# Splitting the last row of a ReLU row sum into three column pieces instead of two

## The chip, the cores and the metric

The kernel runs on one core of a Trainium2 chip. The metric is the time of one execution on the device in microseconds (us). Besides it each run lists its **span**: the time from the program's first to its last instruction in the profile, rounded to 0.1 us. In the lines of the profile DVE is VectorE, ACT is ScalarE, SPq is SyncE's queue, and L102 is line 102 of the kernel that ran. All runs told of here were in the fast state, with a granted clock of 1.00.

## The reference

```python
x = np.random.randn(32, 512, 1024).astype(np.float32)
def reference(x):
    return np.sum(np.maximum(x, 0), axis=-1).astype(np.float32)
```

There are 16384 rows of 1024 numbers, 67 MB, and one number comes out per row. Each of the 128 partitions takes 128 rows.

## The kernel before

SyncE issues all loads on one queue: seven chunks of 16 rows per partition, then a tail that gets smaller (8, 4, 2 and 1 rows), then the last row in two halves. Six chunks are worked on in three steps, ScalarE applying the ReLU and VectorE summing the rows. From the seventh on (and for four rows of the sixth) the engines share the rows: each takes every second one and does both the ReLU and the sum in one call, which becomes an arithmetic instruction and an accumulator read (for a full row 1215 and 83 ns on VectorE, 1044 and 186 ns on ScalarE, means of the trace).

```python
def on_act(t, acc):
    return act.activation(t, t, AF.Relu, accum_out=acc)
def on_dve(t, acc):
    return dve.tensor_scalar(out=t, in0=t, scalar1=0.0, scalar2=None,
                             op0=ALU.max, op1=ALU.add, accum_out=acc)
# ... six chunks in three steps ...
        for i, n in enumerate(steps):
            t = buf[:, b, r : r + n, :]
            act.activation(t, t, AF.Relu).then_inc(s_act, 1)
            dve.wait_ge(s_act, 3 * c + i + 1)
            dve.tensor_reduce(out=res[...], in_=t, axis=X, op=ALU.add).then_inc(s_dve, 1)
# ... the seventh chunk ...
        for i in range(BIG):
            ins = (on_act if i % 2 else on_dve)(*row(c, i))
# ... the tails of 8, 4, 2, 1; then the last row ...
    act.wait_ge(s_in[-2], 16)
    on_act(buf[:, tb, BIG - 1, 0 : LAST[0]], last[:, LAST[1] : LAST[1] + 1]).then_inc(s_tact, 1)
    dve.wait_ge(s_tact, 1)
    dve.wait_ge(s_in[-1], 16)
    on_dve(last[:, :], res[:, J - 1 : J]).then_inc(s_tdve, 1)
    sp.wait_ge(s_tdve, 1)
    sp.dma_start(out=ov[-1][:, :], in_=res[:, start[-1] : J]).then_inc(s_out, 16)
```

ScalarE sums the first half of the last row and puts the sum, which can't be negative, into the column behind the second half. VectorE's last instruction then sums 512 + 1 numbers, and the final store follows.

Of the kernel before, what the change touches and what calls it, by code (L numbers as in the profile page):

```python
# [2 lines left out]

P = 128
D = 1024
BIG = 16
NTWO = 6
NB = 3
REGIONS = [112, 16]
CHUNKS = [(0, 0), (0, 16), (0, 32), (0, 48), (0, 64), (0, 80), (0, 96)]  # L10
STEPS = [4, 5, 7]
MIXED = [3, 4, 5]
TAIL = [8, 4, 2, 1]
LAST = [512, 512]


def bass_relu_sum_kernel(
    nc: bass.Bass,
    x: bass.AP,
    out: bass.AP,  # L20
):







    fp32 = mybir.dt.float32
    ALU = mybir.AluOpType  # L30
    AF = mybir.ActivationFunctionType
    X = mybir.AxisListType.X

    B, S, _ = x.shape
    J = B * S // P
    NBIG = len(CHUNKS)
    assert BIG * NBIG + sum(TAIL) + 1 == J == sum(REGIONS) and sum(LAST) == D

    xr = x.rearrange("b s d -> (b s) d")
    of = out.rearrange("b s -> (b s)")  # L40
    start = [sum(REGIONS[:i]) for i in range(len(REGIONS))]
    xv = [
        xr[P * s : P * (s + n), :].rearrange("(p j) d -> p j d", p=P)
        for s, n in zip(start, REGIONS)
    ]
    ov = [of[P * s : P * (s + n)].rearrange("(p j) -> p j", p=P) for s, n in zip(start, REGIONS)]

    buf = nc.alloc_sbuf_tensor("buf", [P, NB, BIG, D], fp32)
    last = nc.alloc_sbuf_tensor("last", [P, LAST[1] + 1], fp32)
    res = nc.alloc_sbuf_tensor("res", [P, J], fp32)  # L50

    n_in = NBIG + len(TAIL) + 2
    s_in = [nc.alloc_semaphore(f"s_in{i}") for i in range(n_in)]
    s_act = nc.alloc_semaphore("s_act")
    s_dve = nc.alloc_semaphore("s_dve")
    s_fact = nc.alloc_semaphore("s_fact")
    s_fdve = nc.alloc_semaphore("s_fdve")
    s_tact = nc.alloc_semaphore("s_tact")
    s_tdve = nc.alloc_semaphore("s_tdve")
    s_store = nc.alloc_semaphore("s_store")  # L60
    s_out = nc.alloc_semaphore("s_out")

    sp, act, dve = nc.sync, nc.scalar, nc.vector


    tb = NBIG % NB
    for c in range(NBIG + 1):
        if c >= NB:
            sp.wait_ge(s_dve, 3 * (c - NB + 1))
        if c < NBIG:  # L70
            g, j = CHUNKS[c]
            sp.dma_start(out=buf[:, c % NB, :, :], in_=xv[g][:, j : j + BIG, :]).then_inc(  # L72
                s_in[c], 16
            )
    r = 0
    tail = []
    for i, n in enumerate(TAIL):
        sp.dma_start(out=buf[:, tb, r : r + n, :], in_=xv[-1][:, r : r + n, :]).then_inc(  # L78
            s_in[NBIG + i], 16
        )  # L80
        tail.append((r, n, s_in[NBIG + i]))
        r += n
    sp.dma_start(out=buf[:, tb, r, 0 : LAST[0]], in_=xv[-1][:, BIG - 1, 0 : LAST[0]]).then_inc(
        s_in[-2], 16
    )
    sp.dma_start(out=last[:, 0 : LAST[1]], in_=xv[-1][:, BIG - 1, LAST[0] : D]).then_inc(
        s_in[-1], 16
    )
    sp.wait_ge(s_fact, 1)
    sp.wait_ge(s_fdve, 1)  # L90
    for g in range(len(REGIONS) - 1):
        sp.dma_start(
            out=ov[g][:, :], in_=res[:, start[g] : start[g] + REGIONS[g]]
        ).then_inc(s_store, 16)
# [6 lines that stand above are left out]
        return dve.tensor_scalar(  # L101
            out=t, in0=t, scalar1=0.0, scalar2=None, op0=ALU.max, op1=ALU.add, accum_out=acc  # L102
        )

    def row(c, i):
        return buf[:, c % NB, i, :], res[:, c * BIG + i : c * BIG + i + 1]

    for c in range(NTWO):
        b, steps = c % NB, STEPS if c < NTWO - 1 else MIXED
        act.wait_ge(s_in[c], 16)  # L110
        if steps is MIXED:
            dve.wait_ge(s_in[c], 16)
            for i in (BIG - 4, BIG - 3):
                on_dve(*row(c, i))
        r = 0
# [4 lines that stand above are left out]
            dve.tensor_reduce(  # L120
                out=res[:, c * BIG + r : c * BIG + r + n], in_=t, axis=X, op=ALU.add
            ).then_inc(s_dve, 1)
            r += n
        if steps is MIXED:
            for i in (BIG - 2, BIG - 1):
                on_act(*row(c, i))


    j0 = NBIG * BIG
    for c in range(NTWO, NBIG):  # L130
        act.wait_ge(s_in[c], 16)
        dve.wait_ge(s_in[c], 16)
        for i in range(BIG):
            ins = (on_act if i % 2 else on_dve)(*row(c, i))
            if i >= BIG - 2:
                ins.then_inc(s_fact if i % 2 else s_fdve, 1)
    for r, n, s in tail:
        if n > 1:
            act.wait_ge(s, 16)
        dve.wait_ge(s, 16)  # L140
        for i in range(r, r + n):
            f = on_act if (i - r) % 2 else on_dve
            f(buf[:, tb, i, :], res[:, j0 + i : j0 + i + 1])

    act.wait_ge(s_in[-2], 16)
    on_act(buf[:, tb, BIG - 1, 0 : LAST[0]], last[:, LAST[1] : LAST[1] + 1]).then_inc(s_tact, 1)
    dve.wait_ge(s_tact, 1)
    dve.wait_ge(s_in[-1], 16)
    on_dve(last[:, :], res[:, J - 1 : J]).then_inc(s_tdve, 1)


    sp.wait_ge(s_tdve, 1)
    sp.dma_start(out=ov[-1][:, :], in_=res[:, start[-1] : J]).then_inc(s_out, 16)
    sp.wait_ge(s_store, 16 * (len(REGIONS) - 1))
    sp.wait_ge(s_out, 16)


# [1 line left out]
_INS = ['x']  # L159
_OUTS = [((32, 512), 'float32')]  # L160


# [21 lines left out]
```

## Time and profile before

| What | Before |
|---|---|
| Time, the three runs known at first | 162.46 to 162.5 us, median 162.47 |
| Profiled run | 162.37 us, span 160.7 us |
| Load queue's share of the span | 97.4% |
| VectorE, ScalarE busy | 76%, 63% |
| From VectorE's last full row to the final store | 2.16 us (157.09 to 159.25) |

With the load queue at 97.4% of the span the load stream sets the time, and behind it stands a short tail. The last row of the table is the measure for that tail. It starts at an event just after the landing of the last full row, so it does not depend on when the loads as a whole come to an end.

### The profile page before, as it was taken

To read this page: it belongs to the slowest core of one execution; us is meant where nothing else is said; L and a number is where in the kernel's file an instruction comes from. 1 tells how busy PE (TensorE), PEld (TensorE's weight loads), DVE (VectorE), ACT (ScalarE), POOL (GpSimd) and SP (SyncE) were. 2 spreads that over 40 slices of the span, in tenths; PEclk is the share of its full clock that TensorE was granted. 3 is DMA by queue.
4 is the path that set the end of the run, shared out by engine and by line. 5 is a ranking of instruction groups with operands and counts; after the bars stand their busy time and mean duration, and the time that the engine had idled before them with its cause. 6 is when DMAs were issued, how large, how long until landed. Compare 5 with 4: busy or idle time off the path is not lost.

```text
span 160.7 us, 145 instructions
## 1 busy us (share of the span) xinstructions
DVE 122.0 (76%) x56; ACT 101.0 (63%) x55; POOL 0.2 (0%) x4
## 2 busy tenths in 40 slices
DVE  0000004998969898898969989699899999598995
ACT  3000039991599907997099951999329980496972
POOL 0000000000000000000000000000000000000000
DMA  8969969969969969969969969969969969899993
GB/s 261 522 261 522 522 261 522 522 261 522 522 261 522 522 261 522 522 261 522 522 261 522 522 261 522 522 261 522 522 261 522 506 277 522 367 416 391 418 399 113
DMA packets 2160, 67.18 MB, mean 418 GB/s; under 512 B 496, under 2 KB 496, under 8 KB 880
## 3 DMA queue, kind: packets, MB, share of 16 engines
q1 hardware_dynamic: 2160, 67.18, 97.4%
HBM read 67.11 MB, written 0.07 MB: 418 GB/s over the span
## 4 chain that ended last, share of the span: by engine, by line
DMA 69%; ACT 18%; DVE 10%; SPq 1%; issue 0%
DMA buf<-in_x_dram 69%; ACT buf L118 17%; DVE res L120 9%; SPq L78 1%; ACT buf L98 0%; DVE last L101 0%; SPq L72 0%
## 5 line engine op out<-in xcount | busy, mean ns | idle before, releaser
L120 DVE TENSOR_REDUCE res<-buf 128x4 f32<-128x4096 f32 (+3 forms) x18 | 100.4, 5604 | 34.3 <-ACT buf L118 34.3
L118 ACT ACTIVATE buf<-buf 128x4096 f32<-128x4096 f32 (+3 forms) x18 | 80.8, 4553 | 47.1 <-DMA buf<-in_x_dram 47.1
L98 ACT ACTIVATE buf<-buf 128x1024 f32<-128x1024 f32 (+1 forms) x18 | 18.4, 1021 | 9.7 <-DMA buf<-in_x_dram 9.7
L101 DVE TENSOR_SCALAR_CACHE_REDUCE buf<-buf 128x1024 f32<-128x1024 f32 x18 | 21.0, 1215 | 2.7 <-DMA buf<-in_x_dram 2.5
L98 ACT ACTIVATION_READ_ACCUMULATOR buf<-buf 128x1 f32 x18 | 3.4, 186 | 0.0
L118 ACT ACT_TABLE_LOAD x1 | 1.3, 1283 | 0.7 <-PEq L169 0.7
L101 DVE DVE_READ_ACCUMULATOR buf<-buf 128x1 f32 x18 | 1.5, 83 | 0.0
L101 DVE TENSOR_SCALAR_CACHE_REDUCE last<-last 128x513 f32<-128x513 f32 x1 | 0.7, 690 | 0.2 <-ACT buf L98 0.2
L169 POOL MEMSET const-bfloat16-1.0<- 128x1 bf16 x1 | 0.1, 102 | 0.0
L169 POOL MEMSET const-uint8-127<- 128x1 uint8 x1 | 0.1, 102 | 0.0
L169 POOL MEMSET const-float32-0.0<- 128x1 f32 x1 | 0.1, 99 | 0.2 <-issue 0.2
L169 POOL MEMSET const-float32-1.0<- 128x1 f32 x1 | 0.1, 99 | 0.0
L101 DVE DVE_READ_ACCUMULATOR last<-last 128x1 f32 x1 | 0.1, 83 | 0.0
## 6 DMA issues: line engine op xcount, KB each, us to landing
buf<-in_x_dram SPq DMA_DIRECT2D x1, 4096.0 KB, 26.7
buf<-in_x_dram SPq DMA_DIRECT2D x1, 2048.0 KB, 31.2
buf<-in_x_dram SPq DMA_DIRECT2D x1, 1024.0 KB, 33.2
buf<-in_x_dram SPq DMA_DIRECT2D x1, 512.0 KB, 34.0
buf<-in_x_dram SPq DMA_DIRECT2D x1, 256.0 KB, 34.2
last<-in_x_dram SPq DMA_DIRECT2D x1, 256.0 KB, 34.3
buf<-in_x_dram SPq DMA_DIRECT2D x7, 36.3
out_dram<-res SPq DMA_DIRECT2D x1, 56.0 KB, 10.6
```

Source lines behind the costliest of these rows:

```text
L78: sp.dma_start(out=buf[:, tb, r : r + n, :], in_=xv[-1][:, r : r + n, :]).then_inc(s_in[NBIG + i], 16)
L98: return act.activation(t, t, AF.Relu, accum_out=acc)
L101: return dve.tensor_scalar(out=t, in0=t, scalar1=0.0, scalar2=None, op0=ALU.max, op1=ALU.add, accum_out=acc)
L118: act.activation(t, t, AF.Relu).then_inc(s_act, 1)
L120: dve.tensor_reduce(out=res[:, c * BIG + r : c * BIG + r + n], in_=t, axis=X, op=ALU.add).then_inc(s_dve, 1)
L169: nc = _bacc.Bacc("TRN2", target_bir_lowering=False, num_devices=1)
```

## The change

The intent is to let VectorE start on the last row while ScalarE still works, and to make VectorE's last instruction short. The row arrives as 576, 256 and 192 columns. ScalarE sums the first piece and VectorE the second. VectorE's last instruction sums the third together with the two partial sums.

```diff
-LAST = [512, 512]
+LAST = [576, 256, 192]
...
-    last = nc.alloc_sbuf_tensor("last", [P, LAST[1] + 1], fp32)
+    last = nc.alloc_sbuf_tensor("last", [P, LAST[2] + 2], fp32)
...
+    s_tpart = nc.alloc_semaphore("s_tpart")
... (three loads in place of two, each with its own semaphore)
-    act.wait_ge(s_in[-2], 16)
-    on_act(buf[:, tb, BIG - 1, 0 : LAST[0]], last[:, LAST[1] : LAST[1] + 1]).then_inc(s_tact, 1)
+    n = LAST[2]
+    act.wait_ge(s_in[-3], 16)
+    on_act(parts[0], last[:, n : n + 1]).then_inc(s_tact, 1)
+    dve.wait_ge(s_in[-2], 16)
+    on_dve(parts[1], last[:, n + 1 : n + 2]).then_inc(s_tpart, 1)
+    dve.wait_ge(s_in[-1], 16)
+    dve.wait_ge(s_tpart, 1)
     dve.wait_ge(s_tact, 1)
-    dve.wait_ge(s_in[-1], 16)
     on_dve(last[:, :], res[:, J - 1 : J]).then_inc(s_tdve, 1)
```

More of the change, by code (lines that the diff above doesn't have):

```diff
@@ L48, in bass_relu_sum_kernel @@
     buf = nc.alloc_sbuf_tensor("buf", [P, NB, BIG, D], fp32)
-    last = nc.alloc_sbuf_tensor("last", [P, LAST[1] + 1], fp32)
+    last = nc.alloc_sbuf_tensor("last", [P, LAST[2] + 2], fp32)
     res = nc.alloc_sbuf_tensor("res", [P, J], fp32)
-    n_in = NBIG + len(TAIL) + 2
+    n_in = NBIG + len(TAIL) + len(LAST)
     s_in = [nc.alloc_semaphore(f"s_in{i}") for i in range(n_in)]
@@ L82, in bass_relu_sum_kernel @@
         r += n
-    sp.dma_start(out=buf[:, tb, r, 0 : LAST[0]], in_=xv[-1][:, BIG - 1, 0 : LAST[0]]).then_inc(
-        s_in[-2], 16
-    )
-    sp.dma_start(out=last[:, 0 : LAST[1]], in_=xv[-1][:, BIG - 1, LAST[0] : D]).then_inc(
-        s_in[-1], 16
-    )
+    n0, n1 = LAST[0], LAST[0] + LAST[1]
+    parts = [buf[:, tb, r, 0:n0], buf[:, tb, r, n0:n1], last[:, 0 : LAST[2]]]
+    for k, (lo, hi) in enumerate([(0, n0), (n0, n1), (n1, D)]):
+        sp.dma_start(out=parts[k], in_=xv[-1][:, BIG - 1, lo:hi]).then_inc(
+            s_in[NBIG + len(TAIL) + k], 16
+        )
     sp.wait_ge(s_fact, 1)
```

## The prediction

> **What bounds the kernel now.** I read the page first, for the busy shares and the chain that ended last, then the chain in order of time, and then the timeline of the last microseconds, because the change touches nothing earlier than those. In the page the reader is to see that no compute engine is full (VectorE 76%, ScalarE 63%), while the DMA engines are busy in every slice and the load queue fills 97.4% of the span.
>
> ```profile
> DVE 122.0 (76%) x56; ACT 101.0 (63%) x55; POOL 0.2 (0%) x4
> q1 hardware_dynamic: 2160, 67.18, 97.4%
> HBM read 67.11 MB, written 0.07 MB: 418 GB/s over the span
> ```
>
> So the 67 MB of input set the time. The change moves not a byte of that. What it can touch is the stretch from the landing of the last input to the end. The chain in order of time shows its steps: the last load of the chain lands at 157.74, ScalarE takes 0.73 us for its half row, VectorE 0.69 us for the other half.
>
> ```profile
> 123.55 34.19 DMA buf<-in_x_dram
> 157.74 0.02 issue
> 157.76 0.73 ACT buf L98 x2
> 158.49 0.03 issue
> 158.53 0.69 DVE last L101 x2
> ```
>
> The timeline shows the same stretch with VectorE's row before it, and the store that ends the program.
>
> ```profile
> 157.09 1.22 DVE L101 TENSOR_SCALAR_CACHE_REDUCE buf<-buf 128x1024 f32<-128x1024 f32 x1
> 157.76 0.63 ACT L98 ACTIVATE buf<-buf 128x512 f32<-128x512 f32 x1 [0.83 <-DMA buf<-in_x_dram]
> 158.24 0.08 DVE L101 DVE_READ_ACCUMULATOR buf<-buf 128x1 f32 x1
> 158.30 0.18 ACT L98 ACTIVATION_READ_ACCUMULATOR buf<-buf 128x1 f32 x1
> 158.53 0.69 DVE L101 TENSOR_SCALAR_CACHE_REDUCE last<-last 128x513 f32<-128x513 f32 x1 [0.21 <-ACT buf L98]
> 159.14 0.08 DVE L101 DVE_READ_ACCUMULATOR last<-last 128x1 f32 x1
> 159.25 0.34 SPq L153 DMA_DIRECT2D out_dram<-res  x1
> ```
>
> VectorE is free of its last full row at 158.32 and idles 0.21 us for ScalarE's partial sum. It ends at 159.14 + 0.08 = 159.22; the store is issued at 159.25, takes 1.4 us to land and closes the span. That store is the same in both kernels.
>
> When do the pieces land? Issue times are in the chain (121.71, 122.08, 122.56 and 123.06 for the tails of 8, 4, 2 and 1 rows, 123.55 for the first half) and in the timeline (124.08 for the second half); the DMA view has the time to landing. The sums are 148.4, 153.3, 155.8, 157.06, 157.74 and 158.4. So the second half lands only some 0.1 us before ScalarE's sum is there: transfer and ScalarE are almost balanced already.
>
> ```profile
> buf<-in_x_dram SPq DMA_DIRECT2D x1, 512.0 KB, 34.0
> buf<-in_x_dram SPq DMA_DIRECT2D x1, 256.0 KB, 34.2
> last<-in_x_dram SPq DMA_DIRECT2D x1, 256.0 KB, 34.3
> ```
>
> [...] six loads on one queue, in issue order, and the store of the first 112 results, issued at 147.99 behind them, needs 10.6 us, to about 158.6, just after the last load. [...] one row takes 1.30 us (155.76 to 157.06), half a row 0.68 and then about 0.65. A straight line through 1.30 and 0.68 is 0.62 us per half row plus 0.06 us per transfer; through two rows (2.48) and one (1.30) it is 0.59 plus 0.12. [...] the trace has 1057 ns for 1024 elements after a wait and 629 for 512, that is 428/512 = 0.836 ns. [...]
>
> **The change part by part.**
>
> *Transfers.* One load more on the same queue, its issue (0.44 us of SyncE near 124.5) 33 us before it matters: nothing. Landing, with 0.08 us per transfer and 0.60 us per half row (both chosen between the two lines above): 576 columns 0.08 + 0.675 = 0.76, so 157.82 instead of 157.74; 256 columns 0.08 + 0.30 = 0.38, so 158.20; 192 columns 0.08 + 0.225 = 0.31, so 158.50 instead of 158.4. All input arrives about 0.1 us later.
>
> *ScalarE.* 64 columns more at 0.836 ns is 0.05 us, so 0.78 us for the pair instead of 0.73. Start 157.84, end 158.62, and with the 0.04 us that the trace has from ScalarE's end to VectorE's start, VectorE could go on at 158.66 instead of 158.53. On the path: 0.13 us later.
>
> *VectorE, middle piece.* VectorE's cost per element: 1215 ns for 1024 and 690 for 513 make 525/511 = 1.03 ns. For 256 elements 690 - 257 x 1.03 = 425 ns, up to the end of its accumulator read. It can start when piece two is there (158.22 with the hand-over) and the row before is done. In the trace rows follow each other every 1.14 us, so 157.09 + 1.14 = 158.23. Both come at about the same moment: start 158.25, end 158.67. This fills the 0.21 us in which VectorE idled, and some more.
>
> *VectorE, last piece.* It waits for three things: data (158.50), ScalarE (158.66), its own partial sum (158.67 + 0.04 = 158.71, if a VectorE wait on VectorE costs what the ScalarE hand-over costs). The last is the latest by 0.05. Then 192 + 2 elements: 690 - 319 x 1.03 = 361 ns instead of 690. End 158.71 + 0.36 = 159.07 instead of 159.22.
>
> *Sum.* The last instruction starts 0.18 us later and is 0.33 us shorter: **0.15 us gained** at best, 0.1% of the span.
>
> **The rivals.** *First: the data come later than worked out.* The two small pieces are 1024 and 768 bytes per partition, shorter than anything in this trace's loads (2048 is the shortest), so the fixed part is extrapolated. With 0.12 us per transfer piece two lands at about 158.3 and three at 158.6; VectorE then goes 0.1 us later and the gain shrinks to 0.05 us. To lose against the kernel before, piece two would have to land after 158.35. The trace speaks mildly against that: two 256 KB pieces took 0.68 and 0.65, which shows no heavy fixed cost. *Second: a new wait takes the place of the old one.* VectorE now waits for its own accumulator read before it can start the last piece, and the overlap of 0.08 us that neighbouring rows enjoy is lost. I have counted this at 0.04 us; if it were 0.2 us the gain would be gone and the time the same as before. The 0.03 to 0.04 us in the chain between engines speaks against so much. *Third: the end is hidden anyway.* If the 56 KB store behind the loads, landed at about 158.6, or the fixed store at the end absorbed the difference, nothing would move. The final store is issued on the last sum's semaphore alone and lands 1.4 us later, well after the other, which speaks against it. None of the three makes more than about 0.2 us either way, because the whole stretch between the last landing and the final store is only 0.8 us, and 2% of the time would be 3.2 us.
>
> **Range and chances.** I take 0.12 us of the 0.15, as two of the rivals only take away and none adds: 162.47 - 0.12 = 162.35. The three runs before spread over 0.04 us. The range goes from 162.22 (transfers without any fixed part, 0.25 gained) to 162.55 (late small pieces and a slow own wait, 0.08 lost). Same within 2% is all but certain, 0.99; 0.005 for each side covers a surprise in the load stream that no view hints at.
>
> **What would show it.** In the timeline of the changed kernel: ScalarE's 128x576 at about 157.84 with 0.68 us; a VectorE 128x256 at about 158.25 with 0.42 us; the last, 128x194, at about 158.71 with 0.36 us, idle before it put down to VectorE itself or to ScalarE within 0.05 us; the final store issued at about 159.1. In the DMA view three last landings at 157.8, 158.2 and 158.5. Wrong would be: the 128x256 starting after 158.35 (transfers mis-sized), a gap over 0.1 us between its end and the last instruction (own wait mis-sized), or the bulk of the loads ending at another time than 157.06, against which 0.1 us could not be seen.

The forecast's sum: a last instruction 0.18 us later and 0.33 us shorter makes 0.15 us gained, of which 0.12 are taken, so 162.47 - 0.12 = 162.35 us. The kernel before has no VectorE wait on VectorE, so the 0.04 us for it is the author's estimate, from ScalarE's hand-over.

## The result, and the profile after

The changed kernel took 162.05 us (median of 6 runs, 161.83 to 162.18), against 162.47 us before (6 runs, 162.19 to 162.53). The ratio is 0.9977, with a 95% interval of 0.9964 to 0.999: the same within 2%, and a real gain. Ratios here are the mean time of one kernel's fast runs over the mean of the other's in the same rounds, so they are not quite the ratio of the medians. The gain is larger than the whole 0.15 us that the prediction found in the tail, and 162.05 lies below its range.

This is the end of the changed kernel in its timeline (start, duration, engine, line, operation, and idle time before it in brackets):

```profile
156.93 1.22 DVE L102 TENSOR_SCALAR_CACHE_REDUCE buf<-buf 128x1024 f32<-128x1024 f32 x1
157.70 0.68 ACT L99 ACTIVATE buf<-buf 128x576 f32<-128x576 f32 x1 [0.89 <-DMA buf<-in_x_dram]
158.08 0.08 DVE L102 DVE_READ_ACCUMULATOR buf<-buf 128x1 f32 x1
158.08 0.42 DVE L102 TENSOR_SCALAR_CACHE_REDUCE buf<-buf 128x256 f32<-128x256 f32 x1
158.29 0.19 ACT L99 ACTIVATION_READ_ACCUMULATOR buf<-buf 128x1 f32 x1
158.42 0.08 DVE L102 DVE_READ_ACCUMULATOR buf<-buf 128x1 f32 x1
158.63 0.35 DVE L102 TENSOR_SCALAR_CACHE_REDUCE last<-last 128x194 f32<-128x194 f32 x1
158.91 0.08 DVE L102 DVE_READ_ACCUMULATOR last<-last 128x1 f32 x1
159.02 0.34 SPq L158 DMA_DIRECT2D out_dram<-res  x1
```

The tail is 159.02 - 156.93 = 2.09 us instead of 2.16: only 0.07 us shorter. The chain of waits at the same place has a new piece between VectorE's two sums (DVEq is VectorE's sequencer):

```profile
156.93 1.58 DVE buf L102 x4
158.51 0.05 DVEq L153
158.56 0.07 issue
158.63 0.36 DVE last L102 x2
```

After both sums are there, 0.12 us pass before the last instruction starts; before the change 0.03 us passed there after ScalarE's sum. So the tail explains less than predicted and the time fell by more. The queues on the page of the changed kernel show one thing that the page of before doesn't have, an instruction packet inside the span:

```profile
q1 hardware_dynamic: 2304, 67.18, 97.5%
q14 instruction: 1, 0.01, 0.0%
```

Two more readings point the same way. The times of the six runs lie 1.33 to 1.40 us above their spans, while the profiled run of before lies 1.67 us above its span. Below, some 1.35 us above the span is called the **short end**, and 1.45 us or more the long one. And the DMA records of the packed trace, which go beyond the span while the views don't, hold one late packet of 8192 bytes in either kernel, on q14 and of the kind that they name instruction: before, it starts 1.38 us after the end of the span; after, it starts 0.18 us before the end. The expectations call it a fetch; below it is the **late packet**. The records don't say for which engine it is.

### The profile page after: what moved, and what is told of

Same layout as the page of the kernel before. It is cut to its first block, busy times and chain, and to the rows that moved or that the text cites. A ratio compares the mean times of both kernels' runs of the same rounds, so it can differ in the third digit from the quotient of the medians.

```text
span 160.5 us, 148 instructions
## 1 busy us (share of the span) xinstructions
DVE 122.0 (76%) x58; ACT 101.0 (63%) x55; POOL 0.2 (0%) x4
## 3 DMA queue, kind: packets, MB, share of 16 engines
q1 hardware_dynamic: 2304, 67.18, 97.5%
## 4 chain that ended last, share of the span: by engine, by line
DMA 69%; ACT 18%; DVE 11%; SPq 1%; issue 0%; DVEq 0%
DMA buf<-in_x_dram 69%; ACT buf L119 18%; DVE res L121 10%; DVE buf L102 1%; SPq L79 1%; SPq L73 0%; DVE last L102 0%; DVEq L153 0%
## 5 line engine op out<-in xcount | busy, mean ns | idle before, releaser
L102 DVE TENSOR_SCALAR_CACHE_REDUCE buf<-buf 128x1024 f32<-128x1024 f32 (+1 forms) x19 | 21.3, 1174 | 2.7 <-DMA buf<-in_x_dram 2.5
```

## The experiments

### First job: is the extra gain real, and do the loads or the split make it?

Theory A was drift: the extra gain is chance in the load stream and outside the span. Theory B was a second effect of the change, outside the tail. The first two runs are the two kernels themselves.

**c_before**, the kernel before, unchanged.

> The kernel before against itself, as a control. The changed kernel's profile shows the tail 0.10 us shorter (from the first ScalarE row after the 148 us mark to the final store, shift of the loads taken out), but the times differ by 0.4 us. Theory A (drift of the load stream and of what lies outside the span makes up the rest): this control differs from its own comparison by 0.1 to 0.3 us in some runs, and spans vary by 0.2 us. Theory B (the change itself has a second effect outside the tail): the control stays within 0.05 us, ratio 1.000, and time less span stays 1.67 us as in the profile of before.

Measured: 162.28 us against 162.34 for the runs of before that all kernels of this job are compared with, ratio 0.9994 (0.9982 to 1.0007). No drift of the size in question, though the time above the span was not constant: 1.40 to 1.67 us.

**c_after**, the changed kernel, unchanged.

> The changed kernel again. Theory A: it is 0.1 us faster than before on the same chip, ratio about 0.9993, and the 0.37 us of the first measurement does not come back. Theory B: again 0.3 to 0.4 us faster, with time less span at 1.33 us, against 1.67 for before.

Measured: 161.98 us, ratio 0.9976 (0.9962 to 0.9989), and 1.32 to 1.40 us above the span in all five runs. The gain came back in full, so theory A fell. The profiled run is instructive: its loads came late and its span was 160.9 us, longer than that of before at 160.7, yet its time of 162.29 us was shorter than the 162.37 us of that run of before.

**t_three_loads**: the three loads, but VectorE sums 256 + 192 columns and ScalarE's sum in one instruction.

```diff
... (edit against the changed kernel; s_tpart goes, and pieces two and three both land in last)
-    on_dve(parts[1], last[:, n + 1 : n + 2]).then_inc(s_tpart, 1)
     dve.wait_ge(s_in[-1], 16)
-    dve.wait_ge(s_tpart, 1)
     dve.wait_ge(s_tact, 1)
```

> The three loads (576, 256, 192) and ScalarE's 576 columns, but VectorE sums pieces two and three in one instruction of 449 elements, as before waiting only for data and ScalarE. Taking the tail alone: ScalarE 0.05 to 0.07 us later, VectorE's last 64 x 1.03 ns = 0.07 us shorter: within 0.03 us of before. If the extra load by itself causes the second effect (theory B, by the load), it is 0.25 us or more faster than before.

Measured: 162.54 us, ratio 1.0007 (0.9994 to 1.0019), no instruction packet in the span, and 1.32 to 1.71 us above the span. So the extra load does not cause the second effect. The expectation for the tail missed: it is 2.35 us (157.12 to 159.47), 0.19 us longer than before. Three terms add up to 0.24: the 576 columns land 0.09 us later than 512 do after the row before them, ScalarE takes 0.05 us more for them, and 0.10 us more pass from ScalarE's sum to the last instruction. That instruction is 0.07 us shorter, which leaves 0.17.

**t_two_576**: two loads of 576 and 448 columns.

```diff
-LAST = [512, 512]
+LAST = [576, 448]
```

> Two loads of 576 and 448 columns, everything else as before: no extra load, no extra semaphore. Tail: within 0.03 us of before under either theory. If this one is 0.25 us faster too, neither the extra load nor the extra VectorE instruction causes the second effect.

Measured: 162.39 us, ratio 1.000 (0.9987 to 1.0013), no packet, 1.38 to 1.73 us above the span. The tail is 2.22 us, 0.06 longer than before, where at most 0.03 was expected. From ScalarE's sum to the last instruction it has 0.02 us, where t_three_loads has 0.14. The two differ there only in the waits ahead of that instruction.

### Second job: VectorE's instruction stream

Only the changed kernel had the late packet inside the span, and it is the only one so far with more VectorE instructions: 61 in the trace, event-semaphore instructions included, against 59 in the four others (before, c_before, t_three_loads, t_two_576). Theory C is that with the two more instructions the late packet starts inside the span and the time outside it gets shorter; by what means, it doesn't say. Rival D is that the number of semaphores or loads counts.

**n_dve2**: before, with two redundant waits on VectorE at places where it idles (1.28 and 1.31 us there in the trace of before).

```diff
             dve.wait_ge(s_act, 3 * c + i + 1)
+            if i == 0 and c in (1, 2):
+                dve.wait_ge(s_in[c], 16)
```

> The kernel before with two redundant waits on VectorE in the second and third chunk, where it idles: two instructions more in VectorE's stream, the number that the change adds; tail, loads and semaphores as before. In all traces so far, one 8192-byte instruction fetch starts 1.38 us after the end of the span, with the time 1.6 to 1.7 us above the span in most runs; only in the changed kernel does it start 0.18 us before the end, and there the time is 1.32 to 1.40 us above the span. Theory C [...]: the page shows an instruction packet inside the span, time less span is 1.35 us, and the time is 0.3 us below before, ratio 0.998, though the tail is the same. Rival D (the time outside the span goes by the number of semaphores or of loads): no instruction packet, ratio 1.000.

Measured: 162.04 us, against 162.38 for before in the same job, ratio 0.9986 (0.9974 to 0.9997; two of the 11 runs of before had the short end, told of below). In all six runs 1.31 to 1.39 us above the span. Its page has the packet:

```profile
q1 hardware_dynamic: 2160, 67.18, 97.4%
q14 instruction: 1, 0.01, 0.0%
```

and its tail is that of before, 159.14 - 156.98 = 2.16 us:

```profile
156.98 1.22 DVE L101 TENSOR_SCALAR_CACHE_REDUCE buf<-buf 128x1024 f32<-128x1024 f32 x1
...
158.42 0.69 DVE L101 TENSOR_SCALAR_CACHE_REDUCE last<-last 128x513 f32<-128x513 f32 x1 [0.21 <-ACT buf L98]
159.03 0.08 DVE L101 DVE_READ_ACCUMULATOR last<-last 128x1 f32 x1
159.14 0.34 SPq L155 DMA_DIRECT2D out_dram<-res  x1
```

So two waits that do nothing for the data give most of what the change gave. Rival D fell: loads and semaphores here are those of before.

**n_act2**: the same two instructions, on ScalarE.

```diff
         act.wait_ge(s_in[c], 16)
+        if c in (1, 2):
+            act.wait_ge(s_in[c - 1], 16)
```

> The kernel before with two redundant waits on ScalarE instead of VectorE. Theory C: no instruction packet inside the span, time as before (ratio 1.000 within 0.001). If any two more instructions do it, ratio 0.998.

Measured: 162.23 us, ratio 0.9995 (0.9982 to 1.0009), no packet in the span. Above the span were 1.74, 1.40, 1.38 and 1.58 us. This is a mixed result. The late packet stays behind the span in the profiled run (1.30 us after its end), but two of the other runs show the short end, and I can't say why.

**after_less2**: the changed kernel with one row of the seventh chunk moved from VectorE to ScalarE, so that VectorE's stream has 59 instructions again. At the end of that chunk ScalarE idled for 1.29 us and VectorE for 0.51 us in the traces of both kernels.

```diff
-            ins = (on_act if i % 2 else on_dve)(*row(c, i))
+            ins = (on_act if i % 2 or i == 0 else on_dve)(*row(c, i))
```

> The changed kernel with one row of the seventh chunk moved from VectorE to ScalarE, where both have slack: VectorE's stream is two instructions shorter again, as long as before's; the three pieces and their sums stay. Theory C: no instruction packet inside the span, time less span back at 1.6 to 1.7 us; what remains is the tail's own gain, 0.10 us (ratio 0.9994). Rival D: stays at 0.9976.

Measured: 162.27 us, ratio 1.0001 (0.9989 to 1.0013), no packet in the span, the late packet again 1.38 us after its end, and 1.62 to 1.76 us above the span in all five runs. The tail is still the changed kernel's, 159.13 - 157.05 = 2.08 us. With the count undone, the measured gain is gone. What is left of it, 0.08 us in the tail, is too small for the times to show.

**one_sem**: the changed kernel with one semaphore for both partial sums, waited for first.

```diff
... (s_tpart goes)
-    on_dve(parts[1], last[:, n + 1 : n + 2]).then_inc(s_tpart, 1)
-    dve.wait_ge(s_in[-1], 16)
-    dve.wait_ge(s_tpart, 1)
-    dve.wait_ge(s_tact, 1)
+    on_dve(parts[1], last[:, n + 1 : n + 2]).then_inc(s_tact, 1)
+    dve.wait_ge(s_tact, 2)
+    dve.wait_ge(s_in[-1], 16)
```

> The changed kernel with one semaphore for both partial sums (wait for 2), waited for first, and the data wait second. In the traces the first wait stands on the instruction itself and the others in an event-semaphore instruction ahead of it; in the changed kernel that one takes the two late sums, and 0.13 us pass between the last sum and the last instruction. With the data alone there it can run early: I expect 0.04 us from the middle piece's accumulator read to the last instruction, the final store 0.09 us earlier against the landing of the first piece, and 0.05% off the changed kernel's time (ratio to before 0.9971 against 0.9976). If the gap is VectorE's own wait on itself, it stays at 0.13 us. The instruction packet stays inside the span.

Measured: 162.01 us, ratio 0.9981 (0.9969 to 0.9993), packet inside the span. The gap in front of the last instruction shrank as expected, from 0.12 to 0.02 us, and the tail is 159.16 - 157.13 = 2.03 us. The further 0.05% of the time that was expected does not show (0.9981 here, 0.9976 for the changed kernel). Here is its chain of waits:

```profile
158.65 0.09 DVE buf L101
158.75 0.02 issue
158.77 0.36 DVE last L101 x2
```

VectorE waits for its own sum here too, and it costs 0.02 us. So the 0.12 us of the changed kernel went with the event-semaphore instruction that has the two late conditions (0.05 us for it in the chain above, 0.07 us more to the start), not with VectorE's wait on itself.

### Third job: the threshold, and the candidates side by side

**n_dve1**: one redundant VectorE wait, 60 instructions.

```diff
+            if i == 0 and c == 1:
+                dve.wait_ge(s_in[c], 16)
```

> The kernel before with one redundant wait on VectorE, not two. Theory C as a threshold in VectorE's count of instructions (59 traced in before, 61 in the changed kernel): if it lies at 61, no instruction packet inside the span and time less span 1.6 to 1.7 us; if at 60, the packet is inside and time less span is 1.35 us. Tail as before: 2.16 us from VectorE's last full row to the final store.

Measured: 162.43 us against 162.27, ratio 1.0012 (0.9999 to 1.0024), no packet in the span, 1.55 to 1.92 us above the span. One instruction gives nothing; if anything it costs.

**r_dve2**, **r_after** and **r_one_sem**: the three kernels with 61 VectorE instructions again, unchanged, on one chip.

> The kernel before with two redundant VectorE waits, again, now beside the changed kernel on one chip. Theory C: time less span 1.35 us in all runs; it is slower than the changed kernel only by the tail, 0.08 us (2.16 against 2.08 us from the last full row to the final store).

> The changed kernel again: time less span 1.35 us in all runs, tail 2.08 us; 0.3 to 0.4 us below before where before has its usual 1.65 us outside the span.

> One semaphore for both sums, again beside the changed kernel: gap before the last instruction 0.04 us, tail 2.03 us, so 0.05 us below the changed kernel; that is about the noise of a mean of five runs, so the trace is to decide.

Measured: 162.03, 162.02 and 161.98 us, ratios 0.9987, 0.9985 and 0.9982 (each about 0.0013 to either side), all 1.32 to 1.40 us above the span. The tails are 2.15, 2.08 and 1.99 us. They order the three as expected, but the times differ by less than their scatter. The kernel with one semaphore has the shortest tail of all that ran, and by the times nothing separates it from the changed kernel. The 0.3 to 0.4 us that r_after was to gain came out as 0.25: here the before of this chip was 162.27.

### Fourth job: both sides of the threshold

**n_dve6**: six redundant VectorE waits, 65 instructions, one in each of the six chunks.

```diff
+            if i == 0:
+                dve.wait_ge(s_in[c], 16)
```

> The kernel before with six redundant VectorE waits (65 traced instructions instead of 59), each beside a wait at which VectorE idles anyway. Theory C as a threshold at 61: an instruction packet inside the span, time less span 1.35 us in all runs, tail 2.16 us. If 61 were only a lucky count, time less span is 1.6 us or more.

Measured: 162.49 us against 162.42, ratio 1.0009 (0.9995 to 1.0023). The packet is inside the span, and 1.34 to 1.40 us lie above the span in all five runs, as expected. But the spans are 161.0 to 161.2 us, and the tail is 159.56 - 156.97 = 2.59 us, not 2.16. The timeline shows where:

```profile
158.18 0.19 ACT L98 ACTIVATION_READ_ACCUMULATOR buf<-buf 128x1 f32 x1
158.84 0.69 DVE L101 TENSOR_SCALAR_CACHE_REDUCE last<-last 128x513 f32<-128x513 f32 x1 [0.64 <-ACT buf L98]
```

and the chain of waits shows that nothing recorded held VectorE:

```profile
157.64 0.73 ACT buf L98 x2
158.37 0.46 issue
158.84 0.70 DVE last L101 x2
```

ScalarE's sum was there at 158.37 and the data at 158.31, and still VectorE started only at 158.84, where the same step took 0.03 us in the kernel before. The late packet now starts 1.51 us before the end of the span. So a stall of 0.43 us (0.46 less 0.03) lies on the path that sets the end, and the gain is given back. In the trace it lies between the 63rd and the 64th of VectorE's 65 instructions. The late packet starts at 159.51, 0.67 us after the 64th has started, so that instruction can't have waited for it.

**before_less2**: the kernel before with one row of the seventh chunk moved to ScalarE, 57 VectorE instructions.

> The kernel before with one row of the seventh chunk moved from VectorE to ScalarE (57 traced VectorE instructions instead of 59). Theory C as a threshold: no instruction packet inside the span, time less span 1.6 to 1.7 us in most runs, time within 0.1 us of before.

Its edit is the one of after_less2. Measured: 162.28 us, ratio 0.9994 (0.9981 to 1.0006), no packet in the span, the late packet 1.30 us after its end, 1.44 to 1.69 us above the span. Four of the five runs lie below the 1.6 us that was expected.

### All counts together

| Kernels | VectorE instructions in the trace | Late packet's start, from the end of the span | Time less span |
|---|---|---|---|
| before_less2 | 57 | 1.30 us after | 1.44 to 1.69 us |
| before (43 runs, the profiled one of before not among them) | 59 | 1.38 us after | 39 runs 1.45 to 1.74, four 1.35 to 1.40 us |
| after_less2 | 59 | 1.38 us after | 1.62 to 1.76 us |
| t_three_loads, t_two_576, n_act2 (14 runs) | 59 | 1.30 to 1.39 us after | nine runs 1.58 to 1.74, five 1.32 to 1.40 us |
| n_dve1 | 60 | 1.33 us after | 1.55 to 1.92 us |
| n_dve2, changed kernel, one_sem (37 runs) | 61 | 0.18 to 0.21 us before | 1.31 to 1.40 us |
| n_dve6 | 65 | 1.51 us before | 1.34 to 1.40 us, but the span 0.3 to 0.4 us longer |

What is shown: in these kernels the switch lies between 60 and 61 VectorE instructions, and crossing it takes some 0.25 us off the mean time outside the span (1.61 us over the 43 runs of before, 1.36 over the 37 runs with 61). What is not shown is how the count does this, and whether the stall of n_dve6 and the time outside the span have one cause: no other trace shows such a stall of VectorE, and none says for which engine the late packet is.

What stays open: why four runs of before, two of n_act2, two of t_three_loads and one of t_two_576 had the short end without the extra instructions (none of these was profiled); what happens between 62 and 64 instructions, where nothing ran; and what VectorE waits for in the stall of n_dve6. A second late packet follows the first by 0.12 to 0.31 us in the traces of n_act2, after_less2 and n_dve1, and these three profiled runs have the longest times above the span, 1.74, 1.76 and 1.92 us. That was not followed up.

## Why the prediction was wrong

**The bound**: right. The load queue still fills 97.5% of the span, and nothing but the end moved. The whole stream shifts from run to run: the last full row landed at 157.07 in the profiled run of before, at 156.91 in that of the changed kernel and at 157.37 in c_after. The prediction had named such a shift as something against which 0.1 us could not be seen, and the comparison of tails leaves it out. It also took its noise from three runs within 0.04 us; the six runs of before in the comparison lie within 0.34 us.

**Transfers**: right. After the last full row the three pieces landed in steps of 0.76, 0.37 and 0.28 us, for 0.76, 0.38 and 0.31 predicted. The first rival, late small pieces, did not occur.

**ScalarE and the middle piece**: right. ScalarE's 576 columns took 0.68 us, and VectorE's 256 took 0.42 us and filled its idle time.

**The last piece**: its duration, 0.36 us, was right. Its start was mis-sized. The prediction let it follow the own sum by 0.04 us, if "a VectorE wait on VectorE costs what the ScalarE hand-over costs". In the run 0.12 us passed, above the 0.1 us that it had named as a sign of being wrong. The run with one semaphore shows that the own wait does cost only 0.02; what the prediction didn't count is the event-semaphore instruction that stands ahead of the last sum in the trace and has the two late waits (0.05 us, and 0.07 us to the start). So the tail gained 0.07 to 0.08 us instead of 0.15. The second rival was right that a new wait eats into the gain, though for another reason.

**The step that failed** is the passage from the tail to the time: "162.47 - 0.12 = 162.35", together with "None of the three makes more than about 0.2 us either way". It takes what lies outside the span as constant, and the two more VectorE instructions as costing only their durations. The runs showed that the time outside the span fell, from between 1.45 and 1.74 us in most runs of before to between 1.32 and 1.40 us in all 16 runs of the changed kernel. That is some 0.25 us in the mean, about three times the tail's own gain, and it is undone by taking the two instructions away (after_less2) and had by adding two waits that do nothing (n_dve2). The profile of before hinted at it: the profiled run's time exceeded its span by 1.67 us, and the prediction didn't ask what that stretch was made of.

**The same within 2%** was right, and no rival came near that limit.

## What to carry to other kernels

When a change that should be worth 0.1 us brings 0.4, compare time less span, not only the spans, and try a dummy with the same instruction count before crediting the edit. Where an instruction waits for several semaphores, the first wait in program order stood on the instruction itself in these traces and the others in an event-semaphore instruction ahead of it; here it paid to let the condition that comes last be that first wait (0.03 us in the kernel before), or to merge the late ones into one semaphore (0.12 us down to 0.02 in one_sem). One or two instructions more or less on VectorE decided over some 0.25 us at the end, and four further waits gave the gain back (the 0.43 us of n_dve6), so a gain of this kind is fragile.
